# Attention block with one score pass: the rows' exponentials turned on TensorE

## Chip, cores and metric

One core of a Trainium2 chip runs the whole block as one program. The metric is the device time of one execution in microseconds; a median is over several executions. The profile below is of one further execution.

## What is computed

One layer over 1024 latent positions (a grid of 16 rows by 64 columns, laid out as 8 tiles of 16 x 8) and 256 context positions, all of width 1024. Cut to what matters here:

```python
def _fourier(u, w_four):
    ug = u.reshape(b, l, F_GROUPS, F_GROUP_DIM).astype(jnp.float32)
    y = jnp.real(jnp.fft.fft2(ug, axes=(1, 3))) * ((l * F_GROUP_DIM) ** -0.5)
    return y.reshape(b, l, F_WIDTH).astype(u.dtype) @ w_four

# neighbourhood attention, 8 heads of 64, window 8 rows x 16 columns, plus all context keys
    s_loc = jnp.einsum('brqhd,brkhd->bhrqk', qg, k_rows, ...) * scale
    s_loc = jnp.where(mask[None, None, None], s_loc + bias[None], NEG_INF)
    s_ctx = jnp.einsum('brqhd,bkhd->bhrqk', qg, kc, ...) * scale
    p = jax.nn.softmax(jnp.concatenate([s_loc, s_ctx], axis=-1), axis=-1)
    o = (jnp.einsum('bhrqk,brkhd->brqhd', p[..., :n_loc], v_rows)
         + jnp.einsum('bhrqk,bkhd->brqhd', p[..., n_loc:], vc))

        f_out = _fourier(fx_in, w_four[l]) * jax.nn.silu(fx_gate)
        na_out = _neighbourhood_attention(...) * jax.nn.silu(nx_gate)
        x_new = x + g_x * (jnp.concatenate([f_out, na_out], axis=-1) @ w_out[l])
```

## The kernel before

Operands of products are cut into a high and a low half (type fp32r), so a product takes two or three passes on TensorE. The stages follow one another: normalisation and gates (to about 75 us), the Fourier fold (`fold_products`) and the Fourier map (`turn_columns`, `seq_fourier`, to about 145 us), the context keys and values, attention (from about 200 us), and the output product.

Attention goes over four head pairs `p` of two heads `h`. `project(p)` and `gate_proj(p)` make queries, keys, values and gate of a pair and, like the Fourier half of the output product (`out_fourier`, tile `po`), are *fill*: they run on TensorE wherever the attention has nothing ready. `build(p)` turns queries and keys to columns.

A head has two passes over the scores. The *row pass* (`row_max`, lines 1167 and 1169, eight query tiles `t`) makes scores with queries on partitions in the one PSUM tile `s`; VectorE adds the bias and takes the maximum (line 1174), ScalarE the exponential and the sum (line 1178, tile `pr`), which serve the softmax's sum alone. `end_rows` turns the eight maxima and sums (line 1203), and GpSimd spreads the maxima into a free part of `qs2`, so that the products of the second pass subtract them. The *second pass* (`scores`) has twelve steps a head: four of context keys (8 and 9, 18 and 19; four query tiles each) and eight of latent keys (two or three query tiles), with keys on partitions. A step makes its scores in a PSUM bank `tb` (two products, lines 1251 and 1252), VectorE adds the turned bias `biast` (line 1260; context steps have none), ScalarE takes the exponential `e` and copies its high half `eh`, VectorE or GpSimd subtracts for the low half `el`, and two value products follow (lines 1283 to 1288). `finish(p)` spreads one over the sums (`rb`) into the gate.

All queues are written out by hand. A planner runs while the program is built: it keeps a clock per engine with modelled durations (`a_t`, `d_t`, `p_t`) and puts each instruction into its engine's in-order queue when it thinks the operands ready; generators (`seq_rows`, `seq_scores`, `seq_products` ...) are asked in the order of the list `seqs`, and fill is taken when none has work. DMAs go through SP's queue (helper `dma`, line 114), at the place where the planner stood, and wait there for the buffer that they overwrite. `tbs` counts the two free `tb` banks, which also take the turned queries and keys, the maxima and `rb`; `flow` holds up to `EHB` steps whose value products are still to come. `start_rows` loads the one `bias` buffer of a head. Helpers `split` (line 111) and `split_by` (line 199) make low halves, `copy_by` (line 204) high ones.

In `turn_columns` VectorE adds the Fourier output weights `wfr` (lines 685, 687) and both halves of them are cut there (lines 686 to 690), ahead of the halves `ph`, `pl` of the columns that `seq_fourier` multiplies.

## Time and profile before

| | us |
|---|---|
| three runs, median (lowest to highest) | 603.55 (602.17 to 604.94) |
| the profiled execution, its own time | 602.94 |
| its span, first to last instruction | 600.4 |
| TensorE busy | 556.8 (93%) |
| VectorE busy | 419.3 (70%) |
| ScalarE busy | 360.6 (60%) |
| GpSimd busy | 201.2 (34%) |

Busy time is counted from an instruction's start to its end; on TensorE successive products overlap, so the pace of a stream is read from start to start. An engine that waits at the head of its queue holds all that stands behind it. `PE` is TensorE, `PEld` its weight load, `DVE` VectorE, `ACT` ScalarE, `POOL` GpSimd, `SPq` the queue that issues DMAs. A transpose is a product with the identity and shows as a MATMUL with `ident`.

### The profile page before, as it was taken

The page shows a single profiled execution, that of the slowest core. Times are in us where ns is not written, and L with a number is a line of the kernel's source. Part 1 is how long each engine was busy: PE and PEld are TensorE (multiplying, and loading weights), DVE is VectorE, ACT ScalarE, POOL GpSimd, SP SyncE. Part 2 cuts the span into 40 slices and gives each one's busy share as a digit, 9 for nine tenths or more (in the row PEclk, how much of TensorE's full clock was granted, in tenths as well). Part 3 has the DMA queues.
Part 4 walks back from the last instruction along what each step waited for, and adds up shares of the span by engine and source line. Part 5 has one row for each costly group of instructions (what it writes and reads, how often), then busy time and mean ns, then how long its engine had stood idle before and what let it go on. Part 6 is the DMA issues. An engine that isn't in the chain of part 4 may idle for free. (4 is left out here: it accounts for less than half of the span.)

```text
span 600.4 us, 8927 instructions
## 1 busy us (share of the span) xinstructions
PE 556.8 (93%) x3123; PEld 480.3 (80%) x3123; DVE 419.3 (70%) x861; ACT 360.6 (60%) x763; POOL 201.2 (34%) x186
## 2 busy tenths in 40 slices
PE   4899999989999999989999999999997688999997
PEld 3667886879879889979778898898896576787886
DVE  5774767586746796767977869868689749688252
ACT  6864543354664586867878677878687546754100
POOL 2200000205704444373344534445426426513300
PEclk9999999999999999999999999999999899999999
DMA  8990065336551313030231210320114364112152
GB/s 331 410 407 13 1 207 178 108 109 184 182 154 70 97 53 107 22 89 0 85 84 40 71 41 10 118 81 22 49 37 148 105 224 153 67 45 106 61 188 92
DMA packets 42612, 68.31 MB, mean 114 GB/s; under 512 B 3396, under 2 KB 25284, under 8 KB 41544
## 3 DMA queue, kind: packets, MB, share of 16 engines
q1 hardware_dynamic: 41560, 64.08, 31.7%
q0 software_dynamic: 1008, 3.67, 1.8%
q8 instruction: 24, 0.39, 0.3%
q14 instruction: 20, 0.16, 0.1%
HBM read 58.82 MB, written 8.91 MB: 113 GB/s over the span
## 5 line engine op out<-in xcount | busy, mean ns | idle before, releaser
L827 PE MATMUL pqkv<-wl,xnh 128*128 128x384 f32 x256 | 86.8, 339 | 0.8 <-POOL wl L199 0.5
L827 PE MATMUL pqkv<-wh,xnh 128*128 128x384 f32 x256 | 86.7, 339 | 0.1
L827 PE MATMUL pqkv<-wh,xnl 128*128 128x384 f32 x256 | 86.6, 338 | 0.0
L1174 DVE CUSTOM_DVE_ANT_0 pr<-s,bias 128x640 f32<-128x640 f32 (+1 forms) x64 | 50.4, 787 | 27.0 <-PE s L1169 18.1
L1178 ACT ACTIVATE pr<-pr,tr 128x640 f32<-128x640 f32 (+1 forms) x64 | 51.3, 802 | 25.4 <-DVE tr L1174 24.9
L733 POOL TENSOR_TENSOR hrs<-hss,mhalf 128x4 f32<-128x4 f32 (+1 forms) x34 | 37.3, 1101 | 80.2 <-DVE hss L730 75.3
L199 DVE TENSOR_TENSOR el<-e,eh 128x384 fp32r<-128x384 f32 (+2 forms) x72 | 50.1, 703 | 11.0 <-ACT eh L204 10.7
L204 ACT CAST eh<-e 128x384 fp32r<-128x384 f32 (+2 forms) x96 | 49.5, 529 | 1.3
L827 PEld LDWEIGHTS pqkv<-wl,xnh 128*128 128x128 f32 x256 | 48.1, 188 | 2.4 <-POOL wl L199 0.8
L827 PEld LDWEIGHTS pqkv<-wh,xnh 128*128 128x128 f32 x256 | 48.1, 188 | 1.7 <-ACT wh L204 0.4
L1270 ACT ACTIVATE e<-e 128x384 f32<-128x384 f32 (+1 forms) x64 | 31.5, 497 | 29.6 <-DVE e L1260 29.3
L827 PEld LDWEIGHTS pqkv<-wh,xnl 128*128 128x128 f32 x256 | 48.1, 188 | 0.8
L199 POOL TENSOR_TENSOR el<-e,eh 128x512 fp32r<-128x512 f32 x24 | 31.2, 1298 | 40.9 <-ACT eh L204 40.9
L1260 DVE TENSOR_TENSOR e<-st,biast 128x256 f32<-128x256 f32 (+2 forms) x80 | 33.9, 443 | 14.2 <-PE st L1252 12.4
L1167 PE MATMUL s<-ks,qs 128*128 128x256 f32 (+1 forms) x128 | 30.1, 317 | 12.6 <-DVE tr L1174 11.8
L1167 PEld LDWEIGHTS s<-ks,qs 128*128 128x128 f32 x128 | 22.0, 189 | 21.5 <-DVE tr L1174 18.5
L1251 PE MATMUL st<-qs,ks 128*128 128x512 f32 (+2 forms) x96 | 33.6, 352 | 2.7 <-DVE gate L1310 2.7
L199 POOL TENSOR_TENSOR wl<-wr,wh 128x384 fp32r<-128x384 f32 (+1 forms) x19 | 21.3, 1121 | 43.8 <-ACT wh L204 41.5
L1447 PE MATMUL po<-oh,mh 128*128 128x512 f32 x88 | 31.9, 403 | 1.9 <-DVE gate L855 1.3
L1252 PE MATMUL st<-qs,ks 128*128 128x512 f32 (+2 forms) x96 | 33.3, 347 | 0.0
L1288 PE MATMUL pv<-el,vs 128*128 128x512 f32 (+2 forms) x80 | 28.7, 359 | 0.8 <-DVE el L199 0.5
L1169 PE MATMUL s<-ks,qs 128*128 128x256 f32 (+1 forms) x128 | 28.3, 302 | 0.0
(299 smaller groups left out, 1561.3 us busy)
## 6 DMA issues: line engine op xcount, KB each, us to landing
wd<-in_w_ada_b_dram SPq DMA_DIRECT2D x8, 1024.0 KB, 11.4
wr<-in_w_in_dram SPq DMA_DIRECT2D x40, 192.0 KB, 2.8
wr<-in_w_in_dram SPq DMA_DIRECT2D x24, 256.0 KB, 3.3
x<-in_xb_dram SPq DMA_DIRECT2D x8, 512.0 KB, 8.4
wdg<-in_w_ada_g_dram SPq DMA_DIRECT2D x8, 512.0 KB, 4.0
owr<-in_w_out_dram SPq DMA_DIRECT2D x16, 256.0 KB, 3.0
y<-in_xb_dram SPq DMA_DIRECT2D x8, 512.0 KB, 5.0
out_dram<-y SPq DMA_DIRECT2D x15, 256.0 KB, 2.0
```

Source lines behind the costliest of these rows:

```text
L199: return [(e, time(n), lambda eng=eng: eng.tensor_tensor(out=out, in0=in0, in1=in1, op=op)) for e, eng, time in (both[k] for k in who)]
L204: return [(e, time(n), lambda cp=cp: cp(out, in_)) for e, cp, time in (both[k] for k in who)]
L733: lambda: pool.tensor_tensor(out=rs[:, 0:nh], in0=ss[:, 0:nh], in1=mhalf[:, 0:nh], op=ALU.pow),
L827: mm(o, x[k][:, ts_], w, start=(k == 0 and n == 0), stop=(k == KT - 1 and n == 2))
L1167: mm(o, qs1[h][:, ts_], ks1[h][:, kk], start=st, stop=sp)
L1174: dve.tensor_tensor_reduce(out=pr, in0=sv, in1=bt, scale=-1.0, scalar=3.0e38, op0=ALU.add, op1=ALU.min, accum_out=tr[:, t:t + 1])
L1178: (ACT_, a_t(nl + CTX) + 0.15, lambda: act.activation(pr, pr, AF.Exp, bias=tr[:, t:t + 1], scale=-1.0, accum_out=sm[:, t:t + 1])),
L1251: mm(s, ks1[h][:, kk], qs1[h][:, qq], start=True, stop=False)
L1252: mm(s, ks2[h][:, kk], qs2[h][:, qq], start=False, stop=True)
L1260: dve.tensor_tensor(out=ew[:, u:v], in0=s3[:, u:v], in1=mixes[p, h][0][:, blocks], op=ALU.add)
L1270: ops = [(DVE_, d_t(m), add), give, lambda: done.__setitem__(("add", p, h, kt), 1), (ACT_, a_t(m), lambda: act.activation(ew, ew, AF.Exp))]
L1447: mm(o, mf[k][m][:, ts_], wf[hf][k][w_], start=(k == 0 and n == 0), stop=(k == 3 and n == 2))
```

## The change

The second pass over the scores is gone. The exponentials of the row pass (`pr`, now five buffers `PRB`, kept as `prs`) are turned on TensorE in blocks of 128x128 (`turned`, `probs`), up to four blocks a step into a `tb` bank; ScalarE copies the high half from there and VectorE subtracts for the low half, then the bank is given back. A context step takes two query tiles by two key tiles. The turned bias, its load, the second exponential, the spread maxima (`mrow`, and the clearing of `qs2`) fall away. A row tile may start when the row five before it has been turned; the bias has two buffers; the turning of the sums is a sequence of its own (`seq_ends`). The one-over-sums are spread once for all eight tiles, with two selecting matrices.

In the Fourier part the two additions on `wfr` move into the loop of the fold (behind product `i == 5`), and the cutting of the weights ahead of that of the last row (`w64`).

The diff, cut to its core (left out: tables and arguments of the turned bias, small set-up code, and lines that are only renamed):

```diff
@@ -620,6 +619,9 @@
...
+            if i == 5:
+                dve.tensor_tensor(out=wfr[0], in0=wfr[0], in1=wfr[1], op=ALU.add)
+                dve.tensor_tensor(out=wfr[2], in0=wfr[2], in1=wfr[1], op=ALU.subtract)
...
@@ -661,6 +663,10 @@
...
+        for m in range(2):
+            act.copy(w4h[m], wfr[2 * m])
+        for m in range(2):
+            dve.tensor_tensor(out=w4l[m], in0=wfr[2 * m], in1=f(w4h[m]), op=ALU.subtract)
...
@@ -682,12 +688,6 @@
...
-        dve.tensor_tensor(out=wfr[0], in0=wfr[0], in1=wfr[1], op=ALU.add)
-        act.copy(w4h[0], wfr[0])
-        dve.tensor_tensor(out=wfr[2], in0=wfr[2], in1=wfr[1], op=ALU.subtract)
-        act.copy(w4h[1], wfr[2])
-        for m in range(2):
-            dve.tensor_tensor(out=w4l[m], in0=wfr[2 * m], in1=f(w4h[m]), op=ALU.subtract)
...
@@ -934,12 +934,8 @@
...
-        prev = [("st", p - 1, 1, 11)] if p else []
+        prev = [("s", p - 1, 1, 7)] if p else []
...
-        if p:
-            for h in range(2):
-                chain((POOL_, 1.0, lambda h=h: pool.memset(f(qs2[h])[64 - 64 * h:104 - 64 * h], 0.0)),
-                      lambda h=h: done.__setitem__(("clear", p, h), 1), rank=0)
...
@@ -953,18 +949,19 @@
...
-        yield [("pv", p - 1, 1, 11)] if p else [], False
-        vals[p] = ap1.tile([P, 2, 10, P], R, tag="vs", name="vs")
+        yield [("pv", p - VSB, 1, 11)] if p >= VSB else [], False
+        vals[p] = ap1.tile([P, 2, 10, P], R, tag="vs", bufs=VSB, name="vs")
...
+    PRB, VSB = 5, 1
...
@@ -978,21 +975,26 @@
...
-            pool.memset(f(ks2[h])[b], 1.0)
+            pool.memset(f(ks2[h])[b], 0.0)
...
-        rrow = ap1.tile([104, P], R, name="rrow")
-        dve.memset(f(rrow), 0.0)
-        sel = ap1.tile([104, P], R, name="sel")
-        dve.memset(f(sel), 0.0)
...
-            dve.memset(f(sel)[64 * h:64 * h + 40, HALF[h]], 1.0)
-        bias = ap1.tile([P, 896], F32, name="bias")
-        pool.memset(bias[:, 256:512], 0.0)
+        rrow = [ap1.tile([104, P], R, name=f"rrow{n}") for n in range(2)]
+        for r in rrow:
...
+        half = ap1.tile([104, 2], F32, name="half")
+        sel = [ap1.tile([104, P], R, name=f"sel{z}") for z in range(2)]
...
+            dve.reduce_sum(half[:, z:z + 1], eye[:, 4 * z:4 * z + 4], axis=AX.X)
+            dve.memset(f(sel[z]), 0.0)
...
+                dve.tensor_copy(sel[z][r, HALF[h]], half[r, z:z + 1].broadcast_to([40, 64]))
...
+        biases = [ap1.tile([P, 896], F32, name=f"bias{n}") for n in range(2)]
+        for b in biases:
...
@@ -1143,9 +1145,11 @@
...
-    maxes = {}
+    maxes, prs = {}, {}
...
+        bias = biases[h]
         dma(bias[:, 0:256], bias_ed[hd, 0])
         dma(bias[:, 512:896], bias_in[hd])
...
@@ -1168,14 +1172,15 @@
...
-        pr = ap1.tile([P, 640], F32, tag="pr", bufs=2, name="pr")[:, 0:nl + CTX]
+        done["s", p, h, t] = 1
+        pr = prs[p, h, t] = ap1.tile([P, 640], F32, tag="pr", bufs=PRB, name="pr")[:, 0:nl + CTX]
...
-              (ACT_, a_t(nl + CTX) + 0.15, lambda: act.activation(pr, pr, AF.Exp, bias=tr[:, t:t + 1], scale=-1.0, accum_out=sm[:, t:t + 1])),
+              (ACT_, a_t(nl + CTX) + 0.15, lambda: act.activation(pr, pr, AF.Exp, bias=tr[:, t:t + 1], scale=-1.0, accum_out=sm[:, t:t + 1]), 1),
...
@@ -1186,113 +1191,108 @@
...
+        pt = tb("pm")[0:8, 0:P]
+        pe.transpose(pt, tr[:, 32:40], ident)
...
-        chain((ACT_, 0.15, lambda: act.copy(mrow[r0:r0 + 8], pt[0:8])),
...
-              (POOL_, p_t(1024), lambda: spread(qs2[h][64 - r0:104 - r0], mrow, slice(r0, r0 + 40), 0, 8)),
...
-    STEPS = ((8, 0, 9, 1, 18, 2, 19, 3, 4, 5, 6, 7), (8, 9, 18, 19, 0, 1, 2, 3, 4, 5, 6, 7))
...
-        dma(biast, bias_t[2 * p + h].rearrange("p (k n) -> p k n", n=P))
...
-    EHB = 4
...
-    def scores(p, h, i):
...
+        rexp[p] = ap1.tile([104, 512], R, tag="rexp", name="rexp")
+        on([(POOL_, p_t(512), lambda: spread(rexp[p], rrow[p % 2]))], lambda: done.__setitem__(("rexp", p), 1))
...
+    STEPS = (10, 11, 0, 1, 2, 3, 12, 4, 13, 5, 6, 7)
+    EHB = 3
+    pvs = {}
...
+    def turned(p, h, t, kt):
...
+        edge = t in (0, NB - 1)
+        if kt < NB:
+            c = (kt - max(t - 1, 0)) * P + (0 if edge else CTX)
...
+            c = (kt - NB) * P + (CTX if edge else 0)
+        return prs[p, h, t][:, c:c + P]
...
+    def queries_of(step):
+        return [2 * (step - 10), 2 * (step - 10) + 1] if step > 9 else list(range(max(step - 1, 0), min(step + 2, NB)))
...
+    def last_step(t):
...
+        return STEPS.index(min(t + 1, NB - 1))
...
+    def probs(p, h, i):
+        step = STEPS[i]
+        qs = queries_of(step)
...
+        src = [(t, kt) for kt in (8, 9) for t in qs] if step > 9 else [(t, step) for t in qs]
+        n = len(src)
+        w = slice(1, 1 + n) if step == 4 else slice(0, n)
...
-        mm(s, ks1[h][:, kk], qs1[h][:, qq], start=True, stop=False)
-        mm(s, ks2[h][:, kk], qs2[h][:, qq], start=False, stop=True)
...
+        for j, (t, kt) in enumerate(src):
+            pe.transpose(s[:, j * P:(j + 1) * P], turned(p, h, t, kt), ident)
+        now[0] += 0.107 * n
...
-        def add():
...
-                dve.tensor_tensor(out=ew[:, u:v], in0=s3[:, u:v], in1=mixes[p, h][0][:, blocks], op=ALU.add)
...
-            ops = [(ACT_, a_t(m), lambda: act.activation(ew, s3, AF.Exp)), give]
...
-            ops = [(DVE_, d_t(m), add), give, lambda: done.__setitem__(("add", p, h, kt), 1), (ACT_, a_t(m), lambda: act.activation(ew, ew, AF.Exp))]
-        ops += [copy_by(m, WHO["ec"], eh[:, w], ew), split_by(m, WHO["ce" if kt >= 8 else "el"], el[:, w], ew, f(eh)[:, w]),
...
+        chain((ACT_, a_t(m), lambda: act.copy(eh[:, w], s3)),
+              (DVE_, d_t(m), lambda: dve.tensor_tensor(out=el[:, w], in0=s3, in1=f(eh)[:, w], op=ALU.subtract)), give,
+              *(((DVE_, 0.27, clear),) if step in (3, 4) else ()),
+              lambda: done.__setitem__(("e", p, h, i), 1), rank=1)
...
+        if step in (10, 3):
+            z = int(step == 3)
...
+        if step > 9:
+            now[0] += 1024 / 2400
+            z, c = divmod(step - 10, 2)
+            for y in range(2):
+                for x in (eh, el):
+                    mm(pv[z][:, 256 * c:256 * c + 256], vs[:, h, 8 + y], x[:, 2 * y:2 * y + 2], start=(step == 10 and y == 0 and x is eh), stop=False)
+        elif step in (3, 4):
...
+                mm(pv[0][:, 256:512], vs[:, h, step], x[:, 0:2], start=False, stop=(step == 4 and x is el))
+                mm(pv[1][:, 0:256], vs[:, h, step], x[:, 2:4], start=(step == 3 and x is eh), stop=False)
...
+            q0 = qs[0]
...
-                mm(pv[q0 // 4][:, (q0 % 4) * P:(q0 % 4 + n) * P], vs[:, h, kt], x[:, w], start=(kt == 8 and x is eh), stop=(kt == 7 and x is el))
+                mm(pv[q0 // 4][:, (q0 % 4) * P:(q0 % 4 + n) * P], vs[:, h, step], x[:, w], start=False, stop=(step == 7 and x is el))
...
+        if step in (4, 7):
...
@@ -1477,63 +1477,60 @@
...
+    HEADS = [(p, h) for p in range(4) for h in range(2)]
...
-                last = (p, 0, 7) if h else (p - 1, 1, 7)
...
+        for p, h in HEADS:
+            while p and ("max", p - 1, h, 7) not in done:
+                yield False
+            start_rows(p, h)
+            yield True
...
+    def seq_rows():
+        last = None
+        for p, h in HEADS:
+            while not has(("q", p, h, 0), ("k", p, h, 0), ("k", p, h, 2), ("bias", p, h)):
+                yield False
+            for t in range(NB):
+                while (t > 2 and ("k", p, h, 1) not in done) or (t > 3 and ("q", p, h, 1) not in done) or (last and ("max", *last) not in done):
...
+                r = 16 * p + 8 * h + t - PRB
+                while r >= 0 and ("st", r // 16, r // 8 % 2, last_step(r % 8)) not in done:
+                    yield False
+                row_max(p, h, t)
+                last = (p, h, t)
...
-                while not has(*((("q", p, h, 0), ("k", p, h, 0), ("k", p, h, 2)))) or (p and not has(("rb", p - 1), ("clear", p, h))):
+    def seq_ends():
+        for p, h in HEADS:
+            while not (("rec", p, h) in done and tbs[0] > 0):
+                yield False
+            end_rows(p, h)
+            yield True
...
+    flow, steps = [], []
...
+    def seq_scores():
+        last = None
+        for p, h in HEADS:
+            for i, step in enumerate(STEPS):
+                while not (has(*(("sum", p, h, t) for t in queries_of(step))) and tbs[0] > 0 and len(flow) < EHB):
...
+                while len(steps) >= S["ns"] and ("e", *steps[-S["ns"]]) not in done:
...
-                    while (t > 2 and ("k", p, h, 1) not in done) or (t > 3 and ("q", p, h, 1) not in done) or (t > 1 and ("sum", p, h, t - 2) not in done):
...
+                steps.append((p, h, i))
+                g = probs(p, h, i)
+                next(g)
+                need = [("e", p, h, i), ("v", p, h, 2 if step > 9 else step // 4)]
+                if last and step in (10, 3):
+                    need.append(("ot", *last, 4 if step == 10 else 7))
+                if p and h == 0 and step == 4:
+                    need.append(("fin", p - 1))
+                flow.append((need, g))
...
-                while not (has(("rows", p, h), ("q", p, h, 1), ("k", p, h, 1))):
...
-                    while not (tbs[0] > 0 and len(flow) < EHB and (STEPS[h][i] % 10 >= 8 or ("biast", p, h) in done)):
...
+            last = (p, h)
...
@@ -1576,7 +1573,7 @@
...
-        seqs = [seq_side(), seq_fourier(), seq_context(), seq_bias(), seq_products(), seq_finish(), seq_build(), seq_rows(), seq_scores()]
+        seqs = [seq_side(), seq_fourier(), seq_context(), seq_bias(), seq_products(), seq_finish(), seq_build(), seq_ends(), seq_rows(), seq_scores()]
...
```

## Rows read from the trace of the kernel before

**Rows 1.** Stretches: length; PE, PEld, DVE, ACT, POOL busy us (count); PE's clock; DMA.

```profile
200.00:450.00 250.00, 240.46 (x1357) 220.69 (x1357) 192.41 (x429) 189.38 (x421) 107.04 (x98) 1.00 0.19 56
...
132.00:135.00 3.00, 3.00 (x16) 2.79 (x16) 0.87 (x3) 1.75 (x5) 1.00 (x1) 0.64 0.01 3
450.00:475.00 25.00, 17.18 (x82) 13.52 (x82) 24.10 (x40) 17.33 (x34) 15.01 (x11) 0.98 0.45 152
474.00:476.00 2.00, 1.52 (x4) 1.25 (x5) 1.76 (x4) 0.29 (x2) 1.78 (x1) 0.54 0.00 0
475.00:500.00 25.00, 21.25 (x99) 17.17 (x98) 12.58 (x29) 11.58 (x27) 9.86 (x7) 0.95 0.49 164
```

**Rows 2.** The chain that ended last: start, length in us, what.

```profile
481.01 0.33 SPq L114
...
481.87 4.29 DMA y<-in_xb_dram
...
555.13 41.95 PE of L1626 x195
```

**Rows 3.** TensorE's groups: count | busy us, mean ns | idle us before, releasers.

```profile
L1251 PE MATMUL st<-qs,ks 128*128 128x512 f32 (+2 forms) x96 | 33.6, 352 | 2.7 <-DVE gate L1310 2.7
...
L1167 PE MATMUL s<-ks,qs 128*128 128x256 f32 (+1 forms) x128 | 30.1, 317 | 12.6 <-DVE tr L1174 11.8 <-DVE ks L204 0.7
L1288 PE MATMUL pv<-el,vs 128*128 128x512 f32 (+2 forms) x80 | 28.7, 359 | 0.8 <-DVE el L199 0.5
```

**Rows 4.** Order of time on TensorE: start, length in us, line, tiles, shape, count.

```profile
10.50 3.34 PE L329 MATMUL pt<-ident,x 128*128 128x128 f32 x16 [0.99 <-ACT x L342]
...
18.71 2.10 PE L329 MATMUL pt<-ident,x 128*128 128x128 f32 x16 [1.74 <-ACT x L342]
...
443.73 0.60 PE L917 MATMUL ptk<-ident,raw 128*128 128x128 f32 x4
444.09 0.42 PE L827 MATMUL pqkv<-wh,xnl 128*128 128x384 f32 x1
444.35 0.34 PE L827 MATMUL pqkv<-wh,xnh 128*128 128x384 f32 x1
...
488.72 0.39 PE L1251 MATMUL st<-qs,ks 128*128 128x512 f32 x1
488.95 0.39 PE L1252 MATMUL st<-qs,ks 128*128 128x512 f32 x1
...
494.64 0.34 PE L1251 MATMUL st<-qs,ks 128*128 128x384 f32 x1
494.82 0.34 PE L1252 MATMUL st<-qs,ks 128*128 128x384 f32 x1
```

**Rows 5.** Groups by shape on VectorE and GpSimd, same columns.

```profile
L199 DVE TENSOR_TENSOR el<-e,eh 128x384 fp32r<-128x384 f32 x48 | 32.8, 686 | 5.1 <-ACT eh L204 5.0
L199 POOL TENSOR_TENSOR el<-e,eh 128x512 fp32r<-128x512 f32 x24 | 31.2, 1298 | 40.9 <-ACT eh L204 40.9
...
L1260 DVE TENSOR_TENSOR e<-st,biast 128x384 f32<-128x384 f32 x32 | 17.5, 548 | 4.6 <-PE st L1252 3.0 <-issue 1.3
...
L907 DVE TENSOR_TENSOR qs<-ptq,qs 64x512 fp32r<-64x512 f32 x15 | 10.3, 689 | 1.7 <-ACT qs L906 1.4
```

**Rows 6.** TensorE in order of time, three stalls: [idle us before, releaser].

```profile
131.59 0.39 PE L1039 MATMUL ga<-ph,w4h 128*128 128x258 f32 x1 [2.15 <-DVE pl L111]
...
472.31 0.56 PE L1167 MATMUL s<-ks,qs 128*128 128x384 f32 x2 [3.12 <-DVE tr L1174]
...
488.02 0.56 PE L1167 MATMUL s<-ks,qs 128*128 128x384 f32 x2 [1.56 <-DVE tr L1174]
```

**Rows 7.** Order of time on VectorE where the Fourier weights are prepared.

```profile
118.83 1.51 DVE L111 TENSOR_TENSOR al<-pe,ah 128x260 fp32r<-128x260 f32 x4 [2.77 <-ACT ah L110]
...
123.91 1.23 DVE L685 TENSOR_TENSOR wf<-wf 128x1024 f32<-128x1024 f32 x1
125.06 1.22 DVE L687 TENSOR_TENSOR wf<-wf 128x1024 f32<-128x1024 f32 x1
```

More of the change, by code (lines that the diff above doesn't have):

```diff
@@ L1707, in _bias_tiles @@
     right = np.concatenate([tile_of(7, 6), tile_of(7, 7)], 2)
-    cuts = (left[..., :P], left[..., P:], inner[..., 2 * P:], inner[..., P:2 * P], inner[..., :P], right[..., :P], right[..., P:])
-    return inner, np.stack([left, right], 1), np.concatenate([t.transpose(0, 2, 1) for t in cuts], 2)
+    return inner, np.stack([left, right], 1)
 def _arrange(i):
```

124 lines of the change are left out of this document (25 added, 99 removed).

## Prediction

> **What bounds the kernel now.** I read the stretches of busy time first, then the chain that ended last, then TensorE's groups with the idle time ahead of them, and last the order of time around its longest stalls. From 200 to 450 us TensorE is busy 240.5 of 250 us, VectorE 192.4, ScalarE 189.4, GpSimd 107.0 [rows 1]: TensorE bounds this stretch, and 9.5 us of it are idle. Whatever attention leaves free there, the fill work (projections) takes. From 450 to 500 us, in the last head pair, it is otherwise: TensorE is busy 17.2 and 21.3 of two times 25 us, so 11.6 us idle, and VectorE is full in the first half (24.1) and half empty in the second (12.6) [rows 1]. The chain shows why: a bias load on SP's queue starts at 481.01, when the last row maximum of head 6 has released it; the `y` loads stand behind it and land 4.3 us later [rows 2], and VectorE's in-order `y` addition and row maxima wait for them. From 555 us the last 195 output products run 42 us without a gap [rows 2]. So the time is TensorE's work plus its stalls, and the tail's stalls are the largest ones that the change touches.
>
> **Score pass on TensorE.** Removed: per head 12 steps of two products (four steps 512 wide, six 384, two 256), 96 instructions on each of two lines [rows 3]. Start to start, a 512-wide one takes 488.95 - 488.72 = 0.23 us and a 384-wide one 494.82 - 494.64 = 0.18 [rows 4]; half of the first, 0.115, for 256. Sum: 64 x 0.23 + 96 x 0.175 + 32 x 0.115 = 35.2 us. Added: per head 4 x 4 context blocks and 22 local blocks, 38 transposes of 128x128, 304 in all. Four such transposes of the kernel before start at 443.73, the next product at 444.09, and that one keeps TensorE 0.26 us instead of 0.17, so 0.45 us for four, 0.11 each [rows 4]. 304 x 0.11 = 33.4 us. Difference: **-1.8 us**, on the bounding engine; the floor, without the longer product behind, is 0.09 x 304 = 27.4, so -7.8. The ceiling is 16 transposes in 3.34 us at the kernel's start, 0.21 each [rows 4]: 63.5 us, so +28.3; I take the value from 443.73 since it is interleaved with products as the new ones will be. The value products keep their columns (a context step is four of 256 instead of two of 512).
> The Trainium skill speaks against transposes here: its page TensorE: Matmul & The Clock Gate, Part 4: PE-mode transpose, says that transposes do not count as activity for the clock gate, so that the full clock does not engage. This trace does not bear it out: transposes alone ran from 10.50 at 0.21 us each, and from 18.71, again transposes alone, 16 take 2.10 us, 0.13 each with the gap between two groups of eight [rows 4]. By the page the sum would be the ceiling above; it is a rival below.
>
> **The other engines.** The addition of the turned bias goes (384 wide, 0.55 us), as does the exponential behind it; the high half is now copied, and the low half subtracted, straight from PSUM. The subtraction of the kernel before took 0.69 us at 384 on VectorE and 1.30 at 512 on GpSimd, 24 times [rows 5]; from PSUM the nearest are the 384-wide addition, 0.55, and 0.69 for the 512-wide one of the queries [rows 5]. VectorE: about 32 x 0.69 + 48 x 0.55 + 16 x 0.42 (the two others, scaled) = 55 us against 50 before, less 35 of additions: -30 us. GpSimd loses 31 us of subtractions, the spreading of maxima and its clearing. ScalarE loses 96 exponentials, near 50 us. None of this counts by itself while TensorE bounds; it shortens the waits. The 128x640 row exponential, its maximum and the row products stay as they are. Cover: between 200 and 450 us the fill, 48 products per gate and 192 per projection; if a step were late with no fill in hand, it would cost its whole chain (transposes 0.44, copy 0.6, subtraction 0.69).
>
> **Order and queues.** Before, all eight maxima of a head had to be known, turned and spread on GpSimd before its scores began; now a context step starts as soon as two rows have their exponentials. So value products can start some 20 us earlier in the last pair, where TensorE is idle. The biases have two buffers, a head's load waits for the head two before it instead of the last one, and eight loads of the turned bias leave SP's queue: the wait ahead of 481.01 goes and the `y` loads come at their own time. What is late next in the tail is VectorE's queue, full until 475. Of 11.6 us idle and about 1.5 us lost to a clock of 0.54 from 474 to 476 behind the stall at 472.31 (TensorE had been idle 3.1 us) [rows 1, 6], I take **-10**, bounds -4 (only the stall at 488.02, behind the `y` loads, and its like go [rows 6]) and -13. Of the 9.5 us idle between 200 and 450 I take **-3**, bounds 0 and -9.5: VectorE, ScalarE and GpSimd are emptier, but the handover from maximum to next row over one PSUM tile, 12.6 us idle in all [rows 3], stays.
> New waits: a transpose stands in TensorE's queue behind up to three exponentials of rows, and holds one of two PSUM banks until both halves are out. Queued behind it: row products, value products, fill. Nothing like it is in the trace of before; the nearest is the value product, which waits for ScalarE then VectorE in the same planned order: 0.8 us idle ahead of 80 [rows 3]; the other end is the row product, 12.6 us over 64 rows, 0.20 each [rows 3]. 96 steps: +1 to +19. I take **+3**, near the value product, since the planner places both by the same model.
>
> **Fourier map.** The two additions on `wfr` (1.23 + 1.22 us) [rows 7] stand in VectorE's queue ahead of the halves that the first output product waits for: TensorE idles 2.15 us until 131.59 [rows 6], then the clock falls, 0.64 granted from 132 to 135 [rows 1]; at that share 3 us do the work of 1.9, so about 1.1 to 1.5 us more are lost. In the fold stage they land in a hole: VectorE waits 2.77 us for ScalarE ahead of 118.83 [rows 7], and 2.45 fit. Without that cover they would only return to the same queue. ScalarE's copies come before those of the last row, which wait for nothing then. The gap closes almost fully: what ended the wait came at about 131.5, 2.45 less is 129.1, and the products ahead end near 131.59 - 2.15 = 129.4. **-3**, bounds 0 (if the weights of the first projection, which do not come earlier, take it back) and -4.
>
> **Sum.** -1.8 - 10 - 3 + 3 - 3 = -14.8. The profiled execution took 602.94 us (span 600.4), 0.6 under the median of the runs: 588.1 on its own scale, 588.7 on that of the median; I say **588.5**.
>
> **Rivals.** (a) VectorE holds the tail: with 24.1 of 25 us in use from 450 to 475 the new subtractions can't run before 475 either. For it: that number; against it: 12.4 us free right after and 30 us less work in all. Tail -4 instead of -10, little from the middle: about 596 to 600.
> (b) Slower: the transposes' waits decide. Each of 96 steps holds TensorE's in-order queue until a row's exponential is done. Without that term the sum is -17.8, so it turns at 17.8 / 96 = 0.19 us a step, which is just what a row product pays now [rows 3]. At 0.4, with busy queues on ScalarE: 603.5 - 17.8 + 38 = 624. For it: two banks, chain of three engines; against: value products pay 0.01, and fill stands between.
> (c) Transposes at the half clock, the skill's rule above: +28.3 instead of -1.8, so 618.6. Against it, the 0.13 us from 18.71 [rows 4].
> (d) All stalls go: -4 - 1.8 - 13 - 9.5 + 1 = -27.3, 576.
> (e) Nothing moves: fill takes the earlier slots and stalls elsewhere return; 603.
>
> **Chances.** The forecast (582 to 595) 0.57; (a) 0.16; (d) 0.09; (b) 0.11; (c) 0.02; (e) 0.05. The measurement can tell 0.5% (3 us). Faster: 0.57 + 0.16 + 0.09 = 0.82; same 0.06; slower 0.12. The range reaches from near (d) to just past (a): 576 to 602; it leaves out about 0.05 below and 0.15 above.
>
> **What would show it.** Right: products on the score lines gone and transposes start to start near 0.11 us; idle ahead of them under 4 us in all; no bias load ahead of the `y` loads near 480; TensorE over 44 of 50 us busy between 450 and 500; the gap at 131.59 under 0.5 us and no slow clock behind it; the last products again 42 us, but from about 541. Wrong: transposes with 0.2 us or more idle ahead of each step (b), 0.21 us start to start (c), or VectorE full from 450 to 500 with TensorE idle (a).

## The result and the profile after

The changed kernel takes 575.26 us (575.05 to 577.24) against 603.41 (602.17 to 604.94) in the same series: a ratio of 0.954 with an interval of 0.951 to 0.957, so 28.2 us less where 14.8 were forecast. The time lies 0.7 us below the range; the rival nearest to it is (d), all stalls go. The profiled execution has a span of 573.6 us against 600.4.

First the time is cut at four instructions that both kernels have on TensorE: the first Fourier product (`ga`), the first product of a gate (`png`), the first of the gate rows (`pgr`, the last projection is then done) and the first of the last output products (`of`). The windows between them, before (columns as in [rows 1]):

```profile
131.59:208.40 76.81, 74.27 (x394) 66.36 (x395) 47.79 (x96) 41.20 (x85) 32.59 (x29) 0.98 0.43 133
208.40:447.55 239.15, 229.71 (x1290) 210.17 (x1290) 184.68 (x411) 182.65 (x409) 105.02 (x96) 1.00 0.19 56
447.55:552.82 105.27, 91.80 (x439) 74.42 (x439) 82.09 (x150) 62.92 (x125) 46.22 (x32) 0.98 0.37 125
552.82:600.40 47.58, 44.16 (x205) 36.53 (x203) 18.01 (x25) 3.12 (x5) 6.04 (x5) 1.00 0.31 111
```

and after:

```profile
128.15:206.40 78.25, 74.38 (x396) 66.59 (x395) 49.39 (x102) 42.23 (x86) 32.87 (x30) 0.98 0.46 138
206.40:433.13 226.73, 225.77 (x1439) 215.34 (x1439) 169.52 (x380) 152.24 (x343) 58.75 (x63) 1.00 0.17 49
433.13:526.13 93.00, 85.58 (x465) 71.97 (x465) 71.08 (x120) 47.88 (x94) 36.88 (x26) 1.00 0.39 132
526.13:573.60 47.47, 43.86 (x205) 36.61 (x203) 11.79 (x18) 0.00 (x0) 0.00 (x0) 1.00 0.24 89
```

The start loses 3.4 us (131.59 to 128.15; 2.15 of it is the gap of [rows 6], the rest came earlier, and lies within the spread of that start that is given under Experiments), the second stretch grows by 1.4, the middle loses 12.4, the tail 12.3, the end 0.1: 26.8 together. In the middle TensorE's idle time goes from 9.4 to 1.0 us, in the tail from 13.5 to 7.4. VectorE, ScalarE and GpSimd lose 15.2, 30.4 and 46.3 us in the middle. So nearly half of the gain lies in the middle, where the prediction had put -3 for the stops (its -1.8 and +3, for the score pass and the new waits, lie there and in the tail). The two stretches do not hold quite the same work: the row products on TensorE (tile `s`; length, busy us and count, clock, DMA), before and after,

```profile
208.40:447.60 239.20, 35.71 (x192) 1.00 0.19 56
206.40:433.10 226.70, 37.89 (x204) 1.00 0.17 49
```

show three more of the 64 rows, 12 products, in the middle of after. By the spacings of [rows 4] that is an estimated 1.8 us of work moved there from the tail, so that the middle gained more than its length says and the tail less.

TensorE's waits from 200 us on, by what ended them (us in all, times, longest): the first three of before, then all of after.

```profile
PE s L1167 <- DVE tr L1174: 11.8, 12, 3.1
PE pv L1283 <- DVE eh L1265: 3.0, 3, 1.4
PE st L1251 <- DVE gate L1310: 2.7, 3, 1.2
```

```profile
PE pv L1275 <- DVE el L1262: 2.9, 4, 1.2
PE po L1447 <- DVE y L1453: 1.5, 2, 1.1
PE po L1447 <- DVE gate L855: 1.5, 1, 1.5
PE ptq L903 <- DVE raw L734: 1.4, 1, 1.4
PE s L1171 <- DVE tr L1179: 0.7, 2, 0.4
```

The whole list of before has 22.1 us in 25 stops, that of after 8.0 in 10 (the expectations below count the smallest gaps too: 22.9 and 8.3). The row products, which still follow one another over the one PSUM tile `s`, wait 0.7 us instead of 11.8. Where those waits lie matters: in the middle (208 to 433 us) the first three lines of before, and the only one of after, are

```profile
PE pv L1283 <- DVE eh L1265: 3.0, 3, 1.4
PE s L1167 <- DVE tr L1174: 2.7, 5, 0.7
PE st L1251 <- DVE gate L1310: 2.3, 2, 1.2
```

```profile
PE pv L1275 <- DVE el L1262: 0.6, 2, 0.3
```

So 9.1 of the 11.8 us stood in the tail. In the middle value products waited for VectorE's clearing of a part of `eh`, row products for their maximum, and score products for a bank that VectorE's product of gate and `rb` had yet to read. TensorE's groups of after, as in [rows 3], and the windows that answer to [rows 1]:

```profile
L1251 PE MATMUL st<-ident,pr 128*128 128x128 f32 x304 | 47.3, 272 | 0.1
L1171 PE MATMUL s<-ks,qs 128*128 128x256 f32 (+1 forms) x128 | 29.9, 313 | 0.7 <-DVE tr L1179 0.7
L1285 PE MATMUL pv<-el,vs 128*128 128x384 f32 (+1 forms) x48 | 15.5, 323 | 0.1
```

```profile
450.00:475.00 25.00, 23.00 (x141) 19.51 (x139) 21.77 (x45) 16.34 (x35) 7.83 (x7) 1.00 0.48 172
475.00:500.00 25.00, 23.65 (x138) 20.64 (x139) 19.38 (x38) 12.53 (x26) 10.36 (x9) 1.00 0.46 158
129.00:135.00 6.00, 6.00 (x39) 5.45 (x39) 2.86 (x7) 3.46 (x8) 3.78 (x3) 1.00 0.56 158
```

The 304 transposes wait 0.1 us in all. TensorE is busy 46.7 of the 50 us from 450 to 500, and behind the Fourier gap, which is gone, the granted clock stays at 1.00, its upper level of 2.4 GHz. A step in order of time:

```profile
251.22 0.60 PE L1251 MATMUL st<-ident,pr 128*128 128x128 f32 x4
251.58 0.43 PE L827 MATMUL pqkv<-wh,xnl 128*128 128x384 f32 x1
251.84 0.33 PE L827 MATMUL pqkv<-wh,xnh 128*128 128x384 f32 x1
```

From the four transposes' start to the next one's are 0.36 us, and that product takes 0.26 instead of 0.17: 0.11 each, as read from [rows 4]. The last two links of the chain of waits:

```profile
506.93 19.36 PE po L1447 x84
526.29 43.71 PE of L1623 x204
```

### The profile page after: what moved, and what is told of

Read it like the earlier page. It is cut to its first block, busy times and chain, and to the rows that moved or that the text cites. A ratio compares the mean times of both kernels' runs of the same rounds, so it can differ in the third digit from the quotient of the medians.

```text
span 573.6 us, 9000 instructions
## 1 busy us (share of the span) xinstructions
PE 546.6 (95%) x3299; PEld 483.5 (84%) x3299; DVE 388.5 (68%) x801; ACT 312.6 (55%) x662; POOL 139.9 (24%) x144
## 4 chain that ended last, share of the span: by engine, by line
PE 75%; DVE 8%; ACT 6%; DMA 6%; issue 2%; POOL 2%; SPq 1%; POOLq 0%; DVEq 0%; ACTq 0%
PE pqkv L827 20%; PE of L1623 8%; PE pg L365 7%; PE po L1447 5%; PE st L1251 4%; PE png L849 4%; DMA wr<-in_w_in_dram 3%; PE s L1171 2%; PE s L1173 2%; PE pv L1285 2%; PE pv L1275 2%; DMA x<-in_xb_dram 2%; DMA owr<-in_w_out_dram 2%; PE pc L1133 1%; PE pw L502 1%
## 5 line engine op out<-in xcount | busy, mean ns | idle before, releaser
L827 PE MATMUL pqkv<-wl,xnh 128*128 128x384 f32 x256 | 88.3, 345 | 0.0
L1262 DVE TENSOR_TENSOR el<-st,eh 128x512 fp32r<-128x512 f32 (+2 forms) x96 | 53.5, 572 | 17.0 <-ACT eh L1261 16.3
L1261 ACT CAST eh<-st 128x512 fp32r<-128x512 f32 (+2 forms) x96 | 47.0, 494 | 29.4 <-PE st L1251 25.9
L1179 DVE CUSTOM_DVE_ANT_0 pr<-s,bias 128x640 f32<-128x640 f32 (+1 forms) x64 | 50.2, 784 | 10.6 <-PE s L1173 10.2
L1251 PE MATMUL st<-ident,pr 128*128 128x128 f32 x304 | 47.3, 272 | 0.1
L1251 PEld LDWEIGHTS st<-ident,pr 128*128 128x128 f32 x304 | 37.0, 140 | 2.8 <-DVE el L1262 0.5
L1627 DVE TENSOR_TENSOR y<-y,of 128x512 f32<-128x512 f32 (+1 forms) x17 | 11.1, 656 | 32.3 <-PE of L1623 32.3
L203 ACT CAST wh<-wr 128x384 fp32r<-128x384 f32 (+1 forms) x44 | 22.6, 539 | 12.7 <-DMA wr<-in_w_in_dram 10.6
L198 DVE TENSOR_TENSOR wl<-wr,wh 128x384 fp32r<-128x384 f32 (+1 forms) x29 | 21.5, 754 | 9.6 <-ACT wh L203 7.7
L198 POOL TENSOR_TENSOR wl<-wr,wh 128x384 fp32r<-128x384 f32 (+1 forms) x19 | 20.9, 1104 | 28.9 <-ACT wh L203 15.2
L365 PE MATMUL pg<-xnh,w 128*128 128x512 f32 x96 | 27.3, 406 | 0.0
L838 ACT COPY raw<-pqkv 128x384 f32<-128x384 f32 x32 | 15.3, 478 | 21.4 <-PE pqkv L827 21.1
## 6 DMA issues: line engine op xcount, KB each, us to landing
wd<-in_w_ada_b_dram SPq DMA_DIRECT2D x8, 1024.0 KB, 11.6
```

The lines of the kernel that those rows point to most:

```text
L198: return [(e, time(n), lambda eng=eng: eng.tensor_tensor(out=out, in0=in0, in1=in1, op=op)) for e, eng, time in (both[k] for k in who)]
L365: mm(pg[j][hf], wj, x[i][:, hs], start=(i == 0 and g == 0), stop=(i == KT - 1 and g == 2))
L827: mm(o, x[k][:, ts_], w, start=(k == 0 and n == 0), stop=(k == KT - 1 and n == 2))
L1179: dve.tensor_tensor_reduce(out=pr, in0=sv, in1=bt, scale=-1.0, scalar=3.0e38, op0=ALU.add, op1=ALU.min, accum_out=tr[:, t:t + 1])
L1251: pe.transpose(s[:, j * P:(j + 1) * P], turned(p, h, t, kt), ident)
L1261: chain((ACT_, a_t(m), lambda: act.copy(eh[:, w], s3)), (DVE_, d_t(m), lambda: dve.tensor_tensor(out=el[:, w], in0=s3, in1=f(eh)[:, w], op ...
```

## Experiments

Times are medians; "before" is the kernel before in the same series (602.2 to 603.9). Since the start up to the first Fourier product came out anywhere from 128.2 to 133.6 us in these traces, also between kernels with the same code there, traces are compared by the stretches above. Their lengths in us (the middle from `png` to `pgr`, the tail from `pgr` to `of`):

| kernel | time | middle | tail |
|---|---|---|---|
| before | 603.4 | 239.1 | 105.3 |
| changed | 575.3 | 226.7 | 93.0 |
| e3: four row buffers | 575.5 | 227.9 | 92.2 |
| e4: and GpSimd load | 580.4 | 227.8 | 95.9 |
| e5: and ScalarE, VectorE load | 577.7 | 227.4 | 95.1 |
| e13: all three loads | 585.9 | 234.5 | 95.9 |
| e14: changed, old step chain | 584.3 | 232.3 | 95.3 |
| e15: before, short step chain | 585.2 | 229.0 | 99.5 |

**The Fourier part alone.** e1 is the changed kernel with the old place of the two additions and the cutting of the weights; e2 is the kernel before with the new one.

```diff
-            if i == 5:
-                dve.tensor_tensor(out=wfr[0], in0=wfr[0], in1=wfr[1], op=ALU.add)
-                dve.tensor_tensor(out=wfr[2], in0=wfr[2], in1=wfr[1], op=ALU.subtract)
...
```

> The changed kernel with its Fourier part undone (the two additions on wfr and the cutting of the weights stand again in the column stage). Theory: the part saves the stall ahead of the first output product and the slow clock behind it, 3.9 us between the traces; so 575.3 + 3.9 = 579.2, with a stall of 2.1 to 2.5 us back and a clock well under 1 behind it. Rival: the stretch after it takes the gain back (the weights of the first projection come no earlier): 575 to 576.5.

> The kernel before with the Fourier part of the change alone. Theory: 603.4 - 3.9 = 599.5, and the shift of 3.9 us is still there at the first product of the rows. Rival: taken back before attention or in it, 602 to 604.

Measured: e1 577.9 (+2.7), e2 600.4 against 603.5 (ratio 0.992 to 0.997, -3.2). In e1 the gap is back:

```profile
PE ga L1040 <- DVE pl L110: 2.2, 1, 2.2
```

The -3 of the prediction holds: clearly in e2; e1's four runs spread from 576.2 to 580.7 us. The two parts of the change hardly touch each other.

**The transposes.** e10 turns each block twice.

```diff
-            pe.transpose(s[:, j * P:(j + 1) * P], turned(p, h, t, kt), ident)
+            for _ in range(2):
+                pe.transpose(s[:, j * P:(j + 1) * P], turned(p, h, t, kt), ident)
```

> The changed kernel with each of the 304 transposes issued twice into the same place (work added, output the same), and the planner's clock told so. Theory, TensorE bounds and its stalls do not absorb work: 304 times 0.09 us = +27 us, 602.5. Rival, the stretches have slack beside TensorE (turning is hidden by waits of other engines): +5 to +15 us, 580 to 590.

Measured 605.0, +29.8 on the changed kernel: 0.098 us for each of the 304 more. TensorE bounds, nothing hides them, and at that price the score pass is worth between what the sum gave it (-1.8) and 35.2 - 29.8, -5.4 us. Its group and a window of the middle:

```profile
L1252 PE MATMUL st<-ident,pr 128*128 128x128 f32 x608 | 80.3, 272 | 0.2 <-DVE el L1259 0.2
```

```profile
208.00:330.00 122.00, 121.87 (x821) 116.59 (x821) 88.11 (x193) 80.25 (x180) 28.17 (x31) 1.00 0.16 48
```

**Load on the other engines.** Did the stops go because GpSimd (whose operations lengthen some of VectorE's, see the last section), ScalarE or VectorE have less to do? e3 is the baseline with room for scratch; e4 and e5 put load back that stands in no chain; e12 takes load from GpSimd in the kernel before.

```diff
+        if step > 9 or step == 0:
+            on([(POOL_, p_t(512), lambda: pool.tensor_tensor(out=scr["pool"]..., in0=z4, in1=z4, op=ALU.add))])
```

> The changed kernel with four buffers for rows of scores instead of five; nothing else differs. It is the baseline for the two kernels with added load, which need the room. Theory L (the stalls of TensorE between 208 and 433 us went because VectorE, ScalarE and GpSimd have less to do beside it) and theory S (they went because a step now starts as soon as its own rows are there, with two bias buffers and no wait for a whole head) both expect 574 to 577 us: rows leave the ring sooner than they did. If the fifth buffer was what let rows run ahead, it takes over 580 us.

> The kernel with four row buffers, and 40 additions of 128x512 on GpSimd added during attention, whose result nothing reads: some 52 us of GpSimd by the 1298 ns that one took in the kernel before, which is about what the change took from GpSimd between 208 and 433 us (105.0 to 58.8 us busy). Theory L in its GpSimd form expects 5 to 10 us more than with four buffers alone (582 to 588 us), with TensorE's idle time between 208 and 433 us back from 1 us toward 9 and the mean time of VectorE's maxima longer; theory S expects within 1.5 us of it (574 to 578 us).

> The kernel with four row buffers, and 96 exponentials of 128x256 on ScalarE and 96 additions of 128x256 on VectorE added during attention, whose results nothing reads: by the nearest rows of before (548 ns for 384 wide on ScalarE, 686 ns for 384 wide on VectorE) some 35 to 40 us on each, about what the change took from each. Theory L in its form for these two engines expects 6 to 12 us more than with four buffers alone (582 to 590 us), a part of it in the tail where VectorE ended the waits; theory S expects at most 3 us more (up to 579 us), all of it in the tail.

> The kernel before, in which GpSimd no longer computes the low parts of the exponentials of the context columns; their value products take the high parts twice, so that part of the computation is changed and TensorE's work is the same. It takes 24 to 32 operations of 1298 ns from GpSimd. Theory G (GpSimd's operations lengthen VectorE's, and the maxima behind them come late) expects over half of the 9.4 us of idle time between 208 and 433 us to go, and 590 to 597 us. If GpSimd's share is not what makes the rows wait, TensorE's idle time there stays at 7 us or more and the time is 600 to 605 us.

Measured: e3 575.5, e4 580.4, e5 577.7, e12 606.5 (ratio 1.003 to 1.007). Windows of e4 and of e12:

```profile
208.00:433.00 225.00, 223.82 (x1424) 212.87 (x1423) 176.77 (x384) 151.10 (x339) 87.79 (x88) 1.00 0.16 47
```

```profile
208.00:433.00 225.00, 211.77 (x1181) 192.34 (x1180) 169.43 (x378) 169.10 (x382) 74.18 (x72) 1.00 0.20 59
```

e4 has 1.2 us idle in the middle although VectorE is busy 9.7 us longer than in e3; its loss lies in the tail. e5 has 1.7 us idle there, e3 1.6. e12 has 13.2 us idle with 26 us less of GpSimd than before (100.7 there). No single engine's load explains the middle.

**The order of the work.** e6 has one bias buffer; e7 one bias buffer and eight row buffers; e8 makes a head's steps wait for all eight sums; e16 also makes a pair's rows wait for the end of the pair before.

```diff
-                while not (has(*(("sum", p, h, t) for t in queries_of(step))) and ...
+                while not (has(*(("sum", p, h, t) for t in range(NB))) and ...
```

> The changed kernel with one bias buffer instead of two, so that a head's bias is loaded only after the last maximum of the head before, as in the kernel before. Theory S expects the first maxima of each head to wait again for the load (4.29 us for the y load in the chain of before is the nearest row for one transfer): 15 heads with 0.3 to 0.8 us of it left on TensorE, 580 to 587 us. Theory L expects 575 to 577 us, because the ring of rows lets TensorE do other work meanwhile.

> The changed kernel with one bias buffer and eight row buffers instead of five (two instead of three for the rounded probabilities, for room): a row may be started up to eight rows ahead of the steps. It is the control for the kernel that waits for a whole head. Theory R (the five-deep ring holds the rows back, so that TensorE comes to the next row after VectorE is done with the last) expects the row waits of the kernel before to come back, 3 to 8 us in the middle, 578 to 583 us. Theory S (steps that start row by row give TensorE other work) expects 574 to 577 us.

> The same with one thing more: the twelve steps of a head wait until all eight of its row sums are there, as in the kernel before, where they waited for the turned maxima of the whole head. Theory S expects the idle time of TensorE in the middle stretch to come back, 5 to 12 us against the control, and the tail to lose the overlap of the last head's rows with its steps, 5 to 10 us: 585 to 597 us. If the row-by-row start is not the reason, only the tail moves: 579 to 585 us with the middle stretch idle under 3 us.

> The kernel with eight row buffers whose steps wait for a whole head, with one thing more: the rows of a pair of heads wait until the sums of the pair before have been spread by TensorE, as they did in the kernel before, so that rows, steps and the end of a pair come in the old order. Theory O expects the stops back: 18 us of idle time or more from 200 us on, and 590 to 600 us. Theory C expects the middle stretch to stay under 3 us idle and 579 to 584 us.

Measured: e6 575.2, e7 574.0, e8 579.6, e16 578.5. The middle of e8, with waits for a whole head, has 1.8 us idle:

```profile
208.00:433.00 225.00, 223.18 (x1423) 213.03 (x1422) 166.59 (x372) 154.36 (x344) 56.66 (x60) 1.00 0.16 47
```

Its trace puts only 1.3 us more than e7 into middle and tail, but it is of the fastest of e8's four runs (576.9 to 580.7), and that of e7 of the slowest of its own (572.1 to 577.2), so the 5.6 us between the medians cannot be looked for in these two. The early start of steps, which the prediction made the reason for -10, is not needed for the stops of the middle to go; by the medians of e7, e8 and e16 it is worth some 4 to 6 us of the whole.

Two more tries on the kernel before. e11 models the maximum 0.15 us longer, so that the planner leaves rows more room; e17 gives it a third row buffer, since VectorE's maximum itself waits there for an exponential of an earlier row, as ahead of this one:

```profile
307.79 0.82 DVE L1174 CUSTOM_DVE_ANT_0 pr<-s,bias 128x640 f32<-128x640 f32 x1 [1.06 <-ACT pr L1178]
```

```diff
-        chain((DVE_, d_t(nl + CTX) + 0.02, top, S["rt"]), ...
+        chain((DVE_, d_t(nl + CTX) + 0.17, top, S["rt"]), ...
```

```diff
-        pr = ap1.tile([P, 640], F32, tag="pr", bufs=2, name="pr")
+        pr = ap1.tile([P, 640], F32, tag="pr", bufs=3, name="pr")
...
```

> The kernel before, its instructions the same, with one number of the planner changed: the modelled duration of the row maximum is 0.15 us longer (0.90 instead of 0.755 us for 640 wide, as the trace has it). Theory A, the stalls of the middle came from rows placed too early for VectorE's true time: they shrink by half or more, 595 to 599. Theory B, they come from the structure of two passes (full queues, waits on SP and GpSimd) and not from that number: 601 to 606.

> The kernel before with three buffers for rows of scores instead of two (and three instead of four for the halves of the exponentials, for room). VectorE's maxima no longer wait for ScalarE's exponential of two rows back, 3.4 us of its idle time between 200 and 430 us. If that is a cause by itself, the rows' 11.8 us of waits fall below 8 and the time to 596 to 600 us; if the steps' work decides, it stays within 601 to 606 us.

Measured: e11 603.5 (ratio 0.997 to 1.004), e17 599.3 (0.992 to 0.997), some 3 us less, but the rows of e17 wait as long as before:

```profile
PE s L1167 <- DVE tr L1174: 11.8, 12, 2.3
```

**All loads, and the chain of a step.** e13 puts the three loads back at once. e14 gives the changed kernel the way of a step of before: out of PSUM by VectorE, through ScalarE, then high and low half, on GpSimd for the context. e15 gives the kernel before the short way, both halves straight from PSUM, and leaves out the bias and the exponential of the second pass.

```diff
-        chain((ACT_, a_t(m), lambda: act.copy(eh[:, w], s3)),
-              (DVE_, d_t(m), lambda: dve.tensor_tensor(out=el[:, w], in0=s3, in1=f(eh)[:, w], op=ALU.subtract)), give,
...
+        if step > 9:
+            ops = [(ACT_, a_t(m), lambda: act.copy(ew, s3)), give]
+        else:
+            ops = [(DVE_, d_t(m), lambda: dve.tensor_tensor(out=ew, in0=s3, in1=low, op=ALU.max)), give, (ACT_, a_t(m), lambda: act.copy(ew, ew))]
+        chain(*ops, copy_by(m, WHO["ec"], eh[:, w], ew), split_by(m, WHO["ce" if step > 9 else "el"], el[:, w], ew, f(eh)[:, w]),
...
```

> The changed kernel with four row buffers and one bias buffer (neither moved the time), and both earlier loads at once: 40 additions of 128x512 on GpSimd, 96 exponentials of 128x256 on ScalarE and 96 additions of 128x256 on VectorE, whose results nothing reads. The other engines are then about as busy as in the kernel before. Theory J (their load together makes TensorE stop) expects over 20 us of idle time on TensorE from 200 us on, and 588 us or more. If load that stands in no chain does not matter even so, the two earlier increments add up: 5.0 and 2.3 us, 582 to 584 us, and under 13 us idle.

> The changed kernel with four row buffers and one bias buffer, in which each step takes the way of the kernel before between TensorE's score or transposition and the value product: VectorE moves the 384 or 256 columns out of PSUM where it added the bias, ScalarE copies them where it took the exponential, then the rounded part on ScalarE and the low part on VectorE, for the context columns on GpSimd (the copies change no value). The order of rows and steps stays as in the changed kernel. Theory C (the shorter chain of a step and what it asks of the engines is what removed the stops) expects 18 us or more of idle time on TensorE from 200 us on, with the value products and the rows among those who wait, and 586 to 598 us. If the order is the reason: under 12 us idle and 575 to 582 us.

> The kernel before with the step chain of the changed one: after the score product ScalarE rounds the columns straight out of PSUM and VectorE takes the low part from PSUM. The bias and the exponential of this second pass are left out, so that part of the computation is changed; score products, order of rows and steps, and the waits between them are those of the kernel before. Theory C expects most of the 22.9 us of idle time to go: under 12 us, and 583 to 590 us. Theory O (the order is the reason) expects the rows to wait as before in the middle, 17 us idle or more, and 597 to 603 us.

Measured: e13 585.9, e14 584.3, e15 585.2 against 602.6 (ratio 0.967 to 0.974). Their windows, in this order:

```profile
208.00:433.00 225.00, 219.03 (x1383) 206.55 (x1383) 196.10 (x435) 170.65 (x404) 83.37 (x83) 1.00 0.16 47
```

```profile
208.00:433.00 225.00, 222.02 (x1397) 209.94 (x1396) 175.85 (x396) 181.64 (x405) 78.74 (x76) 0.99 0.16 47
```

```profile
208.00:433.00 225.00, 222.28 (x1277) 208.46 (x1277) 169.38 (x374) 152.77 (x341) 74.28 (x74) 1.00 0.20 59
```

Idle in the middle: 6.0, 3.0 and 2.7 us, where before has 9.4 and the changed kernel 1.0. The three loads cost 10.6 us together, more than the 5.0 and 2.3 apart, but rather through value products that wait for their low half (3.7 us of the middle) than through rows. e15 came out as theory C said, e14 between the two theories: the short chain alone takes 17.3 us from the kernel before, some 60% of the gain, with the score products and the rules of order untouched (the planner fills the queues anew); yet the old chain put into the changed kernel gives back only 9.0. What in the chain does it, its length or the work that it asks of the engines, these runs do not tell apart. In the 225 us of the window e15 also takes 19.0 us from ScalarE, 26.4 from GpSimd and 3.8 from VectorE (before: 171.7, 100.7 and 173.2 busy), while e13, which adds load and no chain, has VectorE 22.9 us busier than before.

With the Fourier part of before throughout (e14 plus the 2.7 us of e1), four corners stand: 603 with old chain and old rest, 585 with the short chain (e15), 587 with the new rest, 578 with both (e1). The short chain is worth 17 to 18 us on the old rest and 9 on the new; the new rest 16 on the old chain and 7 on the short one. Each removes stops that the other would remove too.

e18 adds four row buffers to e15, which still lets its rows wait 9.9 us (7 times, 4.6 the longest), 1.8 of it in the middle.

```diff
-        pr = ap1.tile([P, 640], F32, tag="pr", bufs=2, name="pr")
+        pr = ap1.tile([P, 640], F32, tag="pr", bufs=4, name="pr")
...
```

> The kernel before with the short chain of a step (bias and exponential of the second pass left out) and four buffers for rows of scores instead of two. With the short chain alone it took 585.2 us and the rows still waited 9.9 us, 4.6 the longest. If the two row buffers are what makes them wait, 577 to 581 us and under 4 us of row waits; if it is the late start of the last pair's rows and steps, 584 to 587 us with the row waits near 9 us.

Measured 585.3: no less, though the rows wait 6.9 us:

```profile
PE s L1167 <- DVE tr L1174: 6.9, 5, 3.0
```

So what the new rest gives on top of the short chain lies mostly in the tail (99.5 and 100.3 us in e15 and e18, 93.0 in the changed kernel). There the rows of e15 still wait 8.1 us, where before had 9.1 and the changed kernel has 0.7: the short chain does not remove the row waits of the tail. Its longest, 4.6 us, ends at 459.9: the maximum stands in VectorE's queue behind low halves of the values (`vs`, 128x256, both inputs in SBUF), four of which take 5.75 us from 453.31 while GpSimd works without a pause; in before the same four take 1.42 us, at 469.64, while GpSimd is idle. None of the longer waits of VectorE there (0.6 us and more, 436 to 510 us) ends at a load, so nothing points to the turned bias on SP's queue. Which part of the new rest it is, stays open: e8 and e16, which put two of its waits back one by one in the changed kernel, have tails of 92.3 and 94.2.

**The opening.** The second stretch grew. On TensorE and VectorE of the changed kernel:

```profile
194.05 0.33 PE L903 MATMUL ptq<-ident,raw 128*128 128x128 f32 x1 [2.37 <-DVE raw L734]
```

```profile
187.82 0.16 DVE L980 COPY eye<-ident 104x8 f32<-104x8 f32 x1
188.02 3.27 DVE L982 COPY eye<-ident 8x8 f32<-8x8 f32 x3
193.57 0.42 DVE L734 TENSOR_TENSOR raw<-raw,hrs 128x256 f32<-128x256 f32 x1
```

Most of this block is old. Before has

```profile
192.81 0.17 DVE L983 COPY eye<-ident 104x8 f32<-104x8 f32 x1
193.01 3.28 DVE L985 COPY eye<-ident 8x8 f32<-8x8 f32 x3
197.18 0.43 DVE L734 TENSOR_TENSOR raw<-raw,hrs 128x256 f32<-128x256 f32 x1
```

and waits 1.0 us on TensorE for that norm. Set-up work for the second selecting matrix and sum row makes the block 5.75 us long instead of 4.37, and the norm that TensorE waits for stands behind it. e9 gives the block out in pieces later:

```diff
...
+        for n, (dur, fn) in enumerate(late):
+            at(clock() + 8.0 + 1.5 * n, lambda dur=dur, fn=fn: on([(DVE_, dur, fn)], None, 0))
...
```

> The changed kernel with VectorE's 5.75 us of setting up the attention stage (187.82 to 193.57 us in its trace) given out in pieces from 8 us later on, behind nothing that TensorE waits for, instead of in one block ahead of the norms. The theory that this block is what cost the opening of attention its 3 us (2.37 us of TensorE waiting for the raw norm at 194.05 us, then a clock of 0.89) expects 571.5 to 573.5 us; if the norms are late for another reason, 575 us.

Measured 576.4: no gain. The stretch does shrink from 78.3 to 74.5 us, but the middle grows by 0.6 and the tail by 1.9 (94.9), and the start of this execution, the slowest of five, came 3.2 us later, in code that is the same. Over all traces the stretch is 74.0 to 76.8 us long with the old set-up (7 kernels) and 76.1 to 78.3 with the new (12). The cause of the loss is shown, its worth for the time is not.

## Why the prediction was half right

- **Direction, Fourier part, score pass: right.** -3 against 2.7 and 3.2 measured; 0.11 us per transpose against 0.11 from start to start and 0.098 by doubling. The signs named under what would show it came, only more of them: transposes 0.1 us idle, 46.7 of 50 us busy, no gap, no bias load ahead of the `y` loads near 480 (the last one goes at 463.87); the last products take about 43.7 us, but from 526 instead of 541.
- **"None of this counts by itself while TensorE bounds", with -3 for the middle: wrong, the largest miss.** This is the step that failed. The middle lost 12.4 us, 8.4 of them idle time of TensorE. TensorE bounds by an order fixed ahead of time, in which it stops whenever VectorE or ScalarE is later than planned; 2.7 us idle instead of 9.4 remain there with the short chain alone (e15), 3.0 with the new rest alone (e14).
- **"The handover from maximum to next row over one PSUM tile, 12.6 us idle in all [rows 3], stays": wrong, and misread.** It was the reason for taking only 3 of the 9.5 us, but the 12.6 are those of the whole kernel, and the middle holds 2.7 of them; the tail, with 9.1, was priced apart. The tile stayed and the waits went, 11.8 to 0.7 us: they fell on 12 of 64 rows, where VectorE was late for the maximum, and were not the price of the handover. The short chain alone takes only 1.9 of them (e15), and the new rest with the old chain has none (e14), so the row waits of the tail went with the new rest.
- **+3 for new waits: too much.** 0.1 us ahead of the transposes. The value product, the near row, was the right neighbour, and the row product's 0.20 a step no bound that was ever near. Rival (b) falls with it.
- **Tail -10: near in size (-12.3), in part by luck.** It was taken from 11.6 us of idle time, for the early start of steps and the `y` loads. The tail's idle time fell by 6.1; some 1.8 us are work that moved into the middle, some 2 the clock (estimates). The wait for a `y` load (2.39 us on VectorE ahead of 486.25, 1.56 on TensorE [rows 6]) did go. But one bias buffer, its loads ahead of the `y` loads again, leaves the tail at 92.9 us (e6), whole-head waits leave it at 92.3 in the fastest run of e8, and the short chain alone gives 5.8 of the 12.3 (e15).
- **A stop priced by its idle time alone: too cheap.** Products are 0.39 us long but follow one another at 0.23 [rows 4], so a stop also shows the 0.16 us that lay under the next product: 15 stops fewer are an estimated 2.4 us. The granted clock of the tail rose from 0.98 to 1.00, of 105 us an estimated 2 us. With the idle time (14.5 us in middle and tail), the start and the opening (2.0), the end (0.1) and the score pass (1.8 to 5.4) that makes 22.8 to 26.4 of the 26.8 us between the traces; up to 4 are left unexplained.
- **The opening, +1.4: not foreseen**, though the diff shows the added set-up ahead of the first norms: the wait for the norm grew from 1.0 to 2.4 us.
- **The chances.** Rival (d), all stalls go, had nearly the right size, with 0.09, but not the mechanism: 8.0 of the 22.1 us of stops from 200 us on remain, and overlap, clock and score pass (estimates) fill its sum. That is luck. Its terms were treated as independent; e14 and e15 show that one part of the change, the short chain or the rest, removes most stops of the middle by itself.

On the clock: from 206.40 to 433.13 the granted clock was 1.00, the upper level, with 232 of the transposes inside, and 1.00 with twice as many (e10), so rival (c) is out. The Trainium skill, page TensorE: Matmul & The Clock Gate, Part 4: PE-mode transpose, says that the full clock does not engage for transposes; this trace, where they stand between products, does not agree. Nor was the ceiling of 0.21 us each the price of a slow clock: the granted clock of before was 1.00 from 10 to 13 us, where it was read.

## What to carry to other kernels

Where one engine is nearly full under a fixed order, ask what makes the others late for it: a shorter and lighter chain on them can be worth more than work taken off the full one (17.3 us here against some 2 to 5). Before a wait total is used as a reason for one stretch, look up how much of it lies there. Do not add up such gains, nor take one experiment that undoes a part as its worth: measure a part alone on the old kernel and its absence on the new one, and expect two numbers. Count a stop as its idle time plus the overlap that it breaks and the clock behind it (here some 2 us each over the whole kernel, by estimate).

## What the hardware showed

GpSimd lengthens only some of VectorE's work. The same two groups from 208 to 433 us without the added GpSimd load (e3), then with it (e4):

```profile
L1262 DVE TENSOR_TENSOR el<-st,eh 128x384 fp32r<-128x384 f32 x36 | 19.4, 553 | 7.4 <-ACT eh L1261 7.4
L734 DVE TENSOR_TENSOR raw<-raw,hrs 128x256 f32<-128x256 f32 x23 | 13.6, 600 | 7.2 <-POOL hrs L733 7.1
```

```profile
L1267 DVE TENSOR_TENSOR el<-st,eh 128x384 fp32r<-128x384 f32 x36 | 19.4, 553 | 6.4 <-ACT eh L1266 6.4
L734 DVE TENSOR_TENSOR raw<-raw,hrs 128x256 f32<-128x256 f32 x23 | 19.2, 841 | 7.1 <-POOL hrs L733 7.0
```

The norm, with both inputs in SBUF, goes from 600 to 841 ns in the mean and from 424 to 972 in the median; the low half, with one input in PSUM, stays at 553. The Trainium skill, page GPSIMD Engine Reference, section 1. Specifications, names VectorE instructions with two SBUF inputs as those that contend with GpSimd, and the trace agrees. Read from PSUM the low half takes 549 ns for 384 columns, against the 686 of [rows 5] with both inputs in SBUF:

```profile
L1262 DVE TENSOR_TENSOR el<-st,eh 128x384 fp32r<-128x384 f32 x48 | 26.0, 549 | 6.7 <-ACT eh L1261 6.2
```

It is not shorter in itself. From 208 to 433 us of before, 11 subtractions of the same size with both inputs in SBUF (tile `wl`) take 544 ns at the least, 554 in the median and 1161 at the most: the mean of 686 comes from the long ones, and what the short chain gains here is that its subtraction is not lengthened.
